# A one-core decoder layer: float32r head sums for the removal keys, later background steps, pinned order of the mixer's products

## The chip, the cores and the metric

One core of a Trainium2 chip runs the whole kernel. The metric is device time in microseconds of one execution. The kernel before takes 2249.39 us, the median of 3 runs (2248.35 to 2249.53).

## The reference, cut to what matters

One layer works on x of 256 tokens by 2048 features, all float32:

```python
x = x + 0.5 * swiglu(rms_norm(x, ffn1_norm), w_gate, w_up, w_down)   # D_FF = 5632
x = gated_parallel_mixer(x, ...)
x = memory_cross_attention(x, mem, ...)
x = x + 0.5 * swiglu(rms_norm(x, ffn2_norm), w_gate, w_up, w_down)
return rms_norm(x, final_norm)
```

The mixer multiplies the normed x by `w_in`, splits the columns into attention, rwkv and gates, and merges both branches:

```python
y_attn = sliding_window_attention(q, k, v, sinks)      # 16 heads of 64, window 128
kk = k * k_k
kk = kk / max(sqrt(sum(kk * kk, over a head)), 1e-12)  # the removal keys
k = k * (1 + (a - 1) * k_a)
y = rwkv7_scan(r, decay, k, v, -kk, kk * a)
y_rwkv = (group_norm(y) * ln_w + ln_b + bonus) * g
merged = gate_attn * (y_attn @ w_proj_attn) + gate_rwkv * (y_rwkv @ w_proj_rwkv)
return x + merged @ w_out
```

## The kernel before

Engines are named as the profile names them: PE multiplies matrices, DVE is VectorE, ACT ScalarE, POOL GpSimd, SP the queue that starts most DMAs.

**Products.** Every float32 operand of a weight product is a pair of float32r values, hi and lo. `times()` (L470) issues three matmuls for each 128x512 block: x hi by w hi (L473), x hi by w lo (L474), x lo by w hi (L475). `product()` walks over the depth in units of two 128-row blocks (KU = 2); for each unit it takes the next weights, then for both token halves (t) calls `multiply()` (L477), which is two times `times()`, six matmuls, and then one `bg.tick()`. With `skew`, the last units run first for one half and then for the other, without ticks. `next_item()` divides the weights up to two items ahead: SP loads raw units (four buffers), ACT casts to hi (L396), DVE subtracts to lo (L397), three buffers each. `feat()` transposes tokens to features on PE (L661), `split()` writes a hi/lo pair (L666, L667, the pairs yahi/yalo, yrhi/yrlo, xhi/xlo among them). PSUM has three small pools (acc, mm, tr) through which everything goes.

**The background.** All else in the mixer is written as generators, held in groups (`Interleave`, L56). A tick lets the first one or few generators of each group run to their next `yield`; `idle(n)` yields n times. So the source decides, tick by tick, behind which product matmuls each step's instructions stand in the engines' queues, which are served in order. In the order of the mixer:

- `attend()` (scores, exp, scaling L936, transposes L942, copies to pt L945, sums L950, then ya's split L957 and L958);
- `scaled()` (L847) evicts a product to tokens, `shifted()` transposes them and mixes each column with its predecessor (L982); the block named "small" holds the low-rank columns;
- `removal_keys(h)` for two halves of eight heads: kk (L1074), its square (L1076), two sums over heads by a matmul with the block matrix `bdones` (L1081), sqrt (L1082), maximum (L1084), two reciprocals (L1086), kk scaled (L1088), at (L1092), bt (L1097, L1099), k (L1104), then the matmuls of `lt` (L1118), masked (L1124) and stored to DRAM (`ld`);
- `substitute()` loads the diagonal blocks (`dl`, L1139, four DMAs on SP) and inverts 32x32 triangles by 31 pairs of DVE steps (L1146, L1151);
- four gate blocks: sigmoid (L1168), the attention product `pa`, and its eviction into `ga` (L1171), stored by POOL;
- `receptances()` and `values()` (kh and kl through `halves_of()` L852, L853/L854; `head_sums()` L857, L861; vtok L1205);
- `pairs(h, q)`, the chain: masks by `masked()` (matmuls L1249, DVE mask L1255) in three sets, `mk`, `later`, `mk_next`, and between them the sums L1286, L1301, L1313, L1329, L1345 to L1357;
- `finish(h, i)`: head sums of y squared, sqrt (L1400), reciprocal (L1402), gate matmuls (L1408), scaling (L1412 to L1419), split into yr;
- gate blocks of rwkv (L1441), the product over yr, the merge, the product with `w_out` and its eviction (L1480), from which `n3.block()` takes the cross-attention's norm.

Sums of weights for the second feed-forward are prepared in the same stretch by `stage()`: two loads on SP (L376), four DVE subtractions (L380 to L385), two stores on SP (L388). `at["pool"]` is None in the mixer and set in both feed-forwards. kh, kl, mk, ga, vtok and the stage's su and sg share one ring of 23 buffers (`t4`).

**The end.** In the second feed-forward the last two of the four output blocks come from plain products; each is evicted on DVE (L769), and `done2()` squares it on ACT (L1587) and multiplies the first three blocks by the final gain on POOL (L1589). `rstd()` (L707, L708, L710) and the last scaling (L1601 to L1605) end the kernel.

Of the kernel before, what the change touches and what calls it, by code (L numbers as in the profile page):

```python
# [7 lines left out]
F32 = mybir.dt.float32  # L8
F32R = mybir.dt.float32r
# [6 lines left out]
P = 128  # L16
# [120 lines left out]
def decoder_layer(ctx: ExitStack, tc: tile.TileContext, a: dict, out: bass.AP):  # L137
# [38 lines left out]


# [17 lines left out]
    def mixer_constants(sp):  # L195
# [36 lines left out]
        return abias, mask3, mask_l, bdup, center, bdones, ones_r, keep  # L232
# [98 lines left out]
    at = {"item": 0, "product": 0, "pool": None}  # L331
# [138 lines left out]
    def times(o, x, w, first, last, **how):  # L470

        (xh, xl), (hi, lo) = x, w
        pe.matmul(o, xh, hi, start=first, stop=False, **how)  # L473
        pe.matmul(o, xh, lo, start=False, stop=False, **how)  # L474
        pe.matmul(o, xl, hi, start=False, stop=last, **how)  # L475

    def multiply(o, x, u, k, t, nk):  # L477
        s = slice(t * P, (t + 1) * P)
        for i in range(KU):
            times(  # L480
                o, [x.at(p, k + i)[:, s] for p in range(2)], [w[:, i, :] for w in u],
                k + i == 0, k + i == nk - 1,
            )
# [230 lines left out]
    def feed_forward(sp, x, norm: Norm, wg, wu, wd, done, begin_last=lambda: None, last=False):  # L714
# [13 lines left out]
        for gi, (j0, nj) in enumerate(GROUPS):  # L728
# [35 lines left out]
            for n in (0, 2):  # L764
                if last and end and n:
                    for m in (n, n + 1):
                        pd = product(h, wd, skew=m == 3)
                        for t in range(2):
                            dve.scalar_tensor_tensor(  # L769
                                col(t, m), pd[t][:], 0.5, col(t, m), ALU.mult, ALU.add  # L770
                            )
                        done(m)
                    continue
                down(sp, h, ch, wd, [[col(t, n + i) for i in range(2)] for t in range(2)])
                if end:
                    done(n)
                    done(n + 1)
# [12 lines left out]
    def aligned(sp):  # L790

        sp.tile([P, 16], F32, name="shift")
# [35 lines left out]
    with tc.tile_pool(name="mx", bufs=1, reuse_waits="tile") as sp:  # L828
        aligned(sp)
        abias, mask3, mask_l, bdup, center, bdones, (bdones_r, bdmean), keep = mixer_constants(sp)  # L830
# [138 lines left out]
        def shifted(tok, cols, mus, outs, name):  # L969
            for q in range(0, len(cols), 2):  # L970
# [96 lines left out]
        def removal_keys(h):  # L1067
# [9 lines left out]
            yield  # L1077
            for i in (0, 2):
                b = tr()
                sq2 = sq[:, i : i + 2, :].rearrange("p c t -> p (c t)")  # L1080
                pe.matmul(b[:], bdones[:], sq2, start=True, stop=True)  # L1081
                act.activation(sq2, b[:], AF.Sqrt)  # L1082
                yield
                dve.tensor_scalar(sq2, sq2, 1e-12, None, ALU.max)  # L1084
                for k in range(2):
                    dve.reciprocal(sq[:, i + k, :], sq[:, i + k, :])  # L1086
                    yield from idle(2)
# [23 lines left out]
            for c in range(2):  # L1111
# [18 lines left out]
                yield  # L1130
# [3 lines left out]
        def substitute():  # L1134
            yield from idle(4)
# [28 lines left out]
        for n in range(4):  # L1164
# [4 lines left out]
            pa = product(ya, W["w_proj_attn"])  # L1169
# [23 lines left out]
        def values(h):  # L1193
# [13 lines left out]
            for i in (0, 2):  # L1207
                b = head_sums(
                    bdones_r, [v[:, i : i + 2, :].rearrange("p c t -> p (c t)") for v in kp[h]]
# [52 lines left out]
        def pairs(h, q):  # L1262
# [11 lines left out]
            for c in range(2):  # L1274
                cs_ = slice(c * P, (c + 1) * P)
                if c == 0:
# [3 lines left out]
                    yield  # L1280
# [58 lines left out]
                if c == 0:  # L1339
                    mk_next = masked(h, js, ((0, 1), (1, 1)))  # L1340
                    yield
# [132 lines left out]
        for n in range(4):  # L1474
# [6 lines left out]
            bg.spawn("feat", n3.block(n, s))  # L1481
# [75 lines left out]
    with tc.tile_pool(name="f2", bufs=1, reuse_waits="tile") as sp:  # L1557
        aligned(sp)
# [15 lines left out]

        def reload():
# [6 lines left out]
        ss = stat.tile([P, 2, 4], F32, tag="ss", name="ss")  # L1582

        def done2(n):
            for t in range(2):
                xs = x[:, t, n * 512 : (n + 1) * 512]
                act.activation(junk_t[:], xs, AF.Square, accum_out=ss[:, t, n : n + 1])  # L1587
                if n < 3:
                    pool.tensor_tensor(xs, xs, fin(n), ALU.mult)  # L1589
# [4 lines left out]
        )  # L1594
        for t in range(2):
# [43 lines left out]
```

## Time and profile before

| | before |
|---|---|
| median of 3 runs | 2249.39 us |
| the profiled execution's own time | 2248.79 us |
| its span | 2247.1 us |
| PE busy | 2231.4 us, 99% |
| DVE busy | 1820.5 us, 81% |
| ACT busy | 1245.0 us, 55% |
| POOL busy | 134.9 us, 6% |
| mean clock granted to PE | 0.999 |
| DMA | 461.35 MB, 205 GB/s over the span |

A row of the timeline has the start in us from the span's beginning, the duration in us, the engine, the line, the operation, output<-inputs with their shape, and how many instructions the row joins; in brackets stands the idle time of the engine before it and what ended it. The waits view has the waiting engine with what it writes and its line, the engine and line it waited for, and then the sum of us, the number and the longest.

### The profile page before, as it was taken

Reading aid. Unit: us, or ns where it says so; the run is one execution under the profiler, and the core shown is the slowest. Engines: PE = TensorE matmul, PEld = TensorE weight load, DVE = VectorE, ACT = ScalarE, POOL = GpSimd, SP = SyncE. Lnnn points to the kernel's source line nnn. Section 1 sums busy time; section 2 is a strip of 40 time slices with the busy share of each in tenths; the row PEclk is TensorE's granted clock in tenths of the full one; section 3 lists DMA queues with packets and bytes.
Section 4 is the critical chain, followed back from the end, with each engine's and each line's share of the span. In section 5 each row is a group of like instructions: output and inputs, shape, how many; then the busy total and the mean of one; then the engine's idle time right before and its main releaser. Section 6 shows DMA issues by size and latency. Waiting matters only on the chain.

```text
span 2247.1 us, 28239 instructions
## 1 busy us (share of the span) xinstructions
PE 2231.4 (99%) x10587; PEld 1833.6 (82%) x10587; DVE 1820.5 (81%) x2342; ACT 1245.0 (55%) x1621; POOL 134.9 (6%) x192
## 2 busy tenths in 40 slices
PE   9999999999999999999999999999999999999998
PEld 7888888888888877788888888888888888888886
DVE  7898988998989476977656666547999999999997
ACT  6555555555556567544444446456665466555654
POOL 1000000000001000201320040001000000000002
PEclk9999999999999999999999999999999999999999
DMA  7555555556556544676767576547565566556564
GB/s 264 187 201 197 201 198 202 200 188 212 195 193 201 169 135 150 198 231 207 224 214 263 187 258 227 190 167 272 197 237 204 195 231 218 201 205 221 197 229 146
DMA packets 229225, 461.35 MB, mean 205 GB/s; under 512 B 15227, under 2 KB 17504, under 8 KB 229088
## 3 DMA queue, kind: packets, MB, share of 16 engines
q1 hardware_dynamic: 220512, 433.62, 56.8%
q0 software_dynamic: 8112, 25.12, 3.5%
q8 instruction: 83, 1.36, 0.2%
q10 hardware_dynamic: 464, 0.79, 0.1%
q14 instruction: 54, 0.44, 0.1%
HBM read 435.91 MB, written 23.59 MB: 204 GB/s over the span
## 4 chain that ended last, share of the span: by engine, by line
PE 95%; DVE 2%; DMA 1%; issue 1%; ACT 1%; SPq 0%; POOL 0%; POOLq 0%; DVEq 0%; ACTq 0%
PE acc L473 19%; PE acc L474 19%; PE acc L475 19%; PE mm L475 8%; PE mm L474 8%; PE mm L473 8%; PE tr L661 2%; PE tr L474 2%; PE tr L473 2%; PE tr L475 2%; PE mm L1313 1%; DVE lo L397 1%; PE tr L1249 1%; DMA raw<-in_w_out_dram 0%; PE mm L903 0%
## 5 line engine op out<-in xcount | busy, mean ns | idle before, releaser
L396 ACT CAST hi<-raw 128x1024 fp32r<-128x1024 f32 (+1 forms) x770 | 756.5, 992 | 714.4 <-PE acc L475 514.8
L397 DVE TENSOR_TENSOR lo<-raw,hi 128x1024 fp32r<-128x1024 f32 (+1 forms) x770 | 886.1, 1153 | 315.5 <-ACT hi L396 314.0
L473 PE MATMUL acc<-hi,xhi 128*128 128x512 f32 (+1 forms) x1166 | 462.2, 397 | 2.1 <-ACT xhi L688 1.7
L474 PE MATMUL acc<-lo,xhi 128*128 128x512 f32 (+1 forms) x1166 | 452.7, 388 | 0.0
L475 PE MATMUL acc<-hi,xlo 128*128 128x512 f32 (+1 forms) x1166 | 452.5, 388 | 0.0
L473 PEld LDWEIGHTS acc<-hi,xhi 128*128 128x128 f32 x1166 | 219.4, 188 | 49.8 <-issue 4.0
L475 PEld LDWEIGHTS acc<-hi,xlo 128*128 128x128 f32 x1166 | 218.8, 188 | 46.0 <-DVE xlo L689 1.0
L474 PEld LDWEIGHTS acc<-lo,xhi 128*128 128x128 f32 x1166 | 219.2, 188 | 43.8 <-issue 1.7
L404 ACT CAST thi<-raw 128x1024 fp32r<-128x1024 f32 x192 | 199.9, 1052 | 62.9 <-DVE raw L427 42.4
L405 DVE TENSOR_TENSOR tlo<-raw,thi 128x1024 fp32r<-128x1024 f32 x192 | 232.2, 1219 | 1.1 <-ACT thi L404 0.4
L474 PE MATMUL acc<-lo,hhi 128*128 128x512 f32 x372 | 145.5, 391 | 0.8 <-DVE lo L397 0.8
L475 PE MATMUL acc<-hi,hlo 128*128 128x512 f32 x372 | 145.5, 391 | 0.0
L473 PE MATMUL mm<-hi,xhi 128*128 128x512 f32 x370 | 145.4, 393 | 0.0
L473 PE MATMUL acc<-hi,hhi 128*128 128x512 f32 x372 | 144.9, 390 | 0.0
L475 PE MATMUL mm<-hi,xlo 128*128 128x512 f32 x370 | 144.3, 390 | 0.0
L474 PE MATMUL mm<-lo,xhi 128*128 128x512 f32 x370 | 144.2, 390 | 0.0
L474 PEld LDWEIGHTS acc<-lo,hhi 128*128 128x128 f32 x372 | 69.9, 188 | 15.4 <-DVE lo L397 1.2
L473 PEld LDWEIGHTS acc<-hi,hhi 128*128 128x128 f32 x372 | 69.9, 188 | 14.3
L475 PEld LDWEIGHTS mm<-hi,xlo 128*128 128x128 f32 x370 | 69.4, 188 | 14.6
L475 PEld LDWEIGHTS acc<-hi,hlo 128*128 128x128 f32 x372 | 69.9, 188 | 14.0
L474 PEld LDWEIGHTS mm<-lo,xhi 128*128 128x128 f32 x370 | 69.5, 188 | 14.2
L473 PEld LDWEIGHTS mm<-hi,xhi 128*128 128x128 f32 x370 | 69.5, 188 | 14.0
(396 smaller groups left out, 3595.7 us busy)
## 6 DMA issues: line engine op xcount, KB each, us to landing
raw<-in_ffn_w_down_dram SPq DMA_DIRECT2D x88, 1024.0 KB, 5.1
raw<-in_ffn_w_gate_dram SPq DMA_DIRECT2D x84, 1024.0 KB, 5.1
raw<-in_ffn_w_up_dram SPq DMA_DIRECT2D x78, 1024.0 KB, 6.2
raw<-in_w_in_dram SPq DMA_DIRECT2D x136, 512.0 KB, 3.5
raw<-in_w_out_dram SPq DMA_DIRECT2D x32, 512.0 KB, 4.4
raw<-sums SPq DMA_DIRECT2D x20, 512.0 KB, 6.3
raw<-in_w_proj_attn_dram SPq DMA_DIRECT2D x16, 512.0 KB, 4.4
raw<-in_w_proj_rwkv_dram SPq DMA_DIRECT2D x16, 512.0 KB, 4.8
```

Of the source, the lines that this page charges most:

```text
L396: at["hi"] = act.copy(hi[:, s], raw[:, s])
L397: at["lo"] = dve.tensor_tensor(lo[:, s], raw[:, s], f32(hi[:, s]), ALU.subtract)
L404: act.copy(hi[:], v[:])
L405: dve.tensor_tensor(lo[:], v[:], f32(hi[:]), ALU.subtract)
L473: pe.matmul(o, xh, hi, start=first, stop=False, **how)
L474: pe.matmul(o, xh, lo, start=False, stop=False, **how)
L475: pe.matmul(o, xl, hi, start=False, stop=last, **how)
L661: pe.transpose(b[:, o : o + P], tok[:, t, col : col + P], ident[:])
L1249: pe.matmul(b[e][:, o : o + P], x1[r, j, cs_], x2[r, j, cs_], start=True, stop=True)
L1313: pe.matmul(vb[:, (o + k) * P : (o + k + 1) * P][:, r], lhs(k, e), rhs[:, k, r], start=first and k + e == 0, stop=True, **ek,)
```

## The change

- The removal keys' squares are split into sh and sl (`halves_of`), and the sums over heads are taken with `head_sums` and the float32r `bdones`, two float32r matmuls in place of one float32 matmul. The float32 `bdones` isn't returned any more. Two ticks pass between the square and the sums, where it was one.
- `shifted()` begins two ticks later for "small". After each store of `lt` two ticks pass in place of one. `substitute()` begins ten ticks after its turn in place of four.
- In `pairs()`, two ticks in place of one pass after `later` and after `mk_next`.
- `multiply()` issues each group of three matmuls after the last matmul of the group before, while `at["pool"]` is None: the order in which the mixer's products are traced is kept.
- The fourth attention product `pa` is skewed. `n3.block()` begins two ticks later.
- In the second feed-forward's last block the eviction goes in halves of 256 columns; ACT squares the first half, DVE the second, into a fifth slot of `ss`, which lies now in the pool's `shift` tile. The gain multiplies are background steps, three ticks later.

```diff
@@ -174,6 +174,10 @@
         for _ in range(n):
             yield
 
+    def later_by(n, steps):
+        yield from idle(n)
+        yield from steps
+
 
     ones = cpool.tile([P, P], F32, name="ones")
     pool.memset(ones[:], 1.0)
@@ -229,7 +233,7 @@
             r = sp.tile([P, P], F32R, name="ones_r" + str(len(ones_r)))
             act.copy(r[:], v[:])
             ones_r.append(r)
-        return abias, mask3, mask_l, bdup, center, bdones, ones_r, keep
+        return abias, mask3, mask_l, bdup, center, ones_r, keep
 
     sinks = cpool.tile([P, 16], F32, name="sinks")
 
@@ -328,7 +332,7 @@
     raws, parts, summed = {}, {}, {}
     first_unused = {items[i][0][1] for i in staged}
     sums_d = dram.tile([len(staged), P, 4, 512], F32, name="sums")
-    at = {"item": 0, "product": 0, "pool": None}
+    at = {"item": 0, "product": 0, "pool": None, "w": None}
 
     def load(u, pieces=None):
 
@@ -472,15 +476,18 @@
         (xh, xl), (hi, lo) = x, w
         pe.matmul(o, xh, hi, start=first, stop=False, **how)
         pe.matmul(o, xh, lo, start=False, stop=False, **how)
-        pe.matmul(o, xl, hi, start=False, stop=last, **how)
+        return pe.matmul(o, xl, hi, start=False, stop=last, **how)
 
     def multiply(o, x, u, k, t, nk):
+
         s = slice(t * P, (t + 1) * P)
         for i in range(KU):
-            times(
-                o, [x.at(p, k + i)[:, s] for p in range(2)], [w[:, i, :] for w in u],
-                k + i == 0, k + i == nk - 1,
-            )
+            with tc.issue_after(at["w"].ins) if at["w"] else nullcontext():
+                w = times(
+                    o, [x.at(p, k + i)[:, s] for p in range(2)], [w[:, i, :] for w in u],
+                    k + i == 0, k + i == nk - 1,
+                )
+            at["w"] = w if at["pool"] is None else None
 
     def combinations(sp, x: Act, seven, name, ready=lambda: True, early=True, n=0):
 
@@ -763,13 +770,18 @@
 
             for n in (0, 2):
                 if last and end and n:
+
+                    whole = [(t, slice(0, 512)) for t in range(2)]
+                    parts_ = [(t, slice(c, c + 256)) for t in range(2) for c in (0, 256)]
+                    pieces = {2: whole, 3: parts_}
                     for m in (n, n + 1):
                         pd = product(h, wd, skew=m == 3)
-                        for t in range(2):
+                        for t, cs in pieces[m]:
                             dve.scalar_tensor_tensor(
-                                col(t, m), pd[t][:], 0.5, col(t, m), ALU.mult, ALU.add
+                                col(t, m)[:, cs], pd[t][:, cs], 0.5, col(t, m)[:, cs],
+                                ALU.mult, ALU.add,
                             )
-                        done(m)
+                            done(m, t, cs)
                     continue
                 down(sp, h, ch, wd, [[col(t, n + i) for i in range(2)] for t in range(2)])
                 if end:
@@ -789,7 +801,7 @@
 
     def aligned(sp):
 
-        sp.tile([P, 16], F32, name="shift")
+        return sp.tile([P, 16], F32, name="shift")
 
 
     with tc.tile_pool(name="f1", bufs=1, reuse_waits="tile") as sp:
@@ -827,7 +839,7 @@
 
     with tc.tile_pool(name="mx", bufs=1, reuse_waits="tile") as sp:
         aligned(sp)
-        abias, mask3, mask_l, bdup, center, bdones, (bdones_r, bdmean), keep = mixer_constants(sp)
+        abias, mask3, mask_l, bdup, center, (bdones, bdmean), keep = mixer_constants(sp)
 
         def t4(name, shape=(P, 4, T), dt=F32):
             return sp.tile(list(shape), dt, tag="t4", name=name, bufs=N4)
@@ -967,6 +979,8 @@
 
 
         def shifted(tok, cols, mus, outs, name):
+            if name == "small":
+                yield from idle(2)
             for q in range(0, len(cols), 2):
                 n = len(cols[q : q + 2])
                 b = feat(tok, cols[q : q + 2])
@@ -1074,11 +1088,13 @@
                 act.activation(kk[:, i, :], kt[h][:, i, :], AF.Copy, scale=nk_k[:, c : c + 1])
             yield
             act.activation(sq[:], kk[:], AF.Square)
-            yield
+            sp_ = halves_of(sq[:], t4("sh", dt=F32R)[:], t4("sl", dt=F32R)[:])
+            yield from idle(2)
             for i in (0, 2):
-                b = tr()
                 sq2 = sq[:, i : i + 2, :].rearrange("p c t -> p (c t)")
-                pe.matmul(b[:], bdones[:], sq2, start=True, stop=True)
+                b = head_sums(
+                    bdones, [v[:, i : i + 2, :].rearrange("p c t -> p (c t)") for v in sp_]
+                )
                 act.activation(sq2, b[:], AF.Sqrt)
                 yield
                 dve.tensor_scalar(sq2, sq2, 1e-12, None, ALU.max)
@@ -1127,12 +1143,12 @@
                     )
                 o = h * 16 + c * 8
                 pool.dma_start(ld[:, o : o + 8, :], lt[:])
-                yield
+                yield from idle(2)
             yield
 
 
         def substitute():
-            yield from idle(4)
+            yield from idle(10)
             dl = t4("dl", (P, 32, 32))
             for i in range(4):
                 q = slice(32 * i, 32 * i + 32)
@@ -1166,7 +1182,7 @@
             g = t4("ga", (P, 2, 512))
             for t in range(2):
                 act.activation(g[:, t, :], pg[t][:], AF.Sigmoid, scale=n2.r[t])
-            pa = product(ya, W["w_proj_attn"])
+            pa = product(ya, W["w_proj_attn"], skew=n == 3)
             for t in range(2):
                 dve.tensor_tensor(g[:, t, :], pa[t][:], g[:, t, :], ALU.mult)
             pool.dma_start(blk(md, n), g[:])
@@ -1206,7 +1222,7 @@
                 yield
             for i in (0, 2):
                 b = head_sums(
-                    bdones_r, [v[:, i : i + 2, :].rearrange("p c t -> p (c t)") for v in kp[h]]
+                    bdones, [v[:, i : i + 2, :].rearrange("p c t -> p (c t)") for v in kp[h]]
                 )
                 v2 = vv[:, i : i + 2, :]
                 dve.tensor_tensor(v2, b[:].rearrange("p (c t) -> p c t", c=2), v2, ALU.mult)
@@ -1277,7 +1293,7 @@
                     mk = masked(h, js, ((0, 0), (1, 0)))
                     yield
                     later = masked(h, js, ((2, 0), (2, 1)))
-                    yield
+                    yield from idle(2)
                 vp = [vtok[h][:, c, j * P : (j + 1) * P] for j in js]
                 x, rr = xb[h, c]
                 b = tr()
@@ -1338,7 +1354,7 @@
                 yield
                 if c == 0:
                     mk_next = masked(h, js, ((0, 1), (1, 1)))
-                    yield
+                    yield from idle(2)
                 b = tr()
                 if c:
                     for k, j in enumerate(js):
@@ -1478,7 +1494,7 @@
             po = product(mt, W["w_out"])
             for t in range(2):
                 dve.tensor_tensor(s[:, t, :], po[t][:], s[:, t, :], ALU.add)
-            bg.spawn("feat", n3.block(n, s))
+            bg.spawn("feat", later_by(2, n3.block(n, s)))
             if n == 0:
                 bg.spawn("mem", memory())
 
@@ -1555,7 +1571,7 @@
 
 
     with tc.tile_pool(name="f2", bufs=1, reuse_waits="tile") as sp:
-        aligned(sp)
+        room = aligned(sp)
         at["pool"] = sp
         x = sp.tile([P, 2, D], F32, name="x")
         fins = []
@@ -1572,6 +1588,11 @@
                 pool.dma_start(fin(n), a["final_norm"][cb].unsqueeze(0).broadcast_to([P, 512]))
                 yield
 
+        def gained(t, n):
+            yield from idle(3)
+            xs = x[:, t, n * 512 : (n + 1) * 512]
+            pool.tensor_tensor(xs, xs, fin(n), ALU.mult)
+
         def reload():
             for n in range(4):
                 cb = slice(n * 512, (n + 1) * 512)
@@ -1579,19 +1600,27 @@
                 pool.dma_start(x[:, :, cb], blk(x3d, n))
 
         bg.spawn("const", reload())
-        ss = stat.tile([P, 2, 4], F32, tag="ss", name="ss")
-
-        def done2(n):
-            for t in range(2):
-                xs = x[:, t, n * 512 : (n + 1) * 512]
-                act.activation(junk_t[:], xs, AF.Square, accum_out=ss[:, t, n : n + 1])
+        ss = room[:, :10].rearrange("p (t n) -> p t n", t=2)
+
+        def done2(n, t=None, cs=slice(0, 512)):
+            for t in range(2) if t is None else (t,):
+                xs = x[:, t, n * 512 : (n + 1) * 512][:, cs]
+                if cs.start:
+                    dve.scalar_tensor_tensor(
+                        junk_t[:, cs], xs, 1.0, xs, ALU.mult, ALU.mult, accum_out=ss[:, t, 4:5]
+                    )
+                else:
+                    act.activation(
+                        junk_t[:, cs], xs, AF.Square, accum_out=ss[:, t, n : n + 1]
+                    )
                 if n < 3:
-                    pool.tensor_tensor(xs, xs, fin(n), ALU.mult)
+                    bg.spawn("ew", gained(t, n))
 
         feed_forward(
             sp, x, n4, W["ffn2_w_gate"], W["ffn2_w_up"], W["ffn2_w_down"], done2,
             begin_last=lambda: bg.spawn("const", gain()), last=True,
         )
+        bg.drain()
         for t in range(2):
             r = rstd(ss[:, t : t + 1, :])[0]
             for n in range(4):
```

## The prediction

> **What bounds the kernel now.** I read the page's span and busy times first, then the chain that ended last, then the PE engine's waits, then windows of the timeline around each place the diff touches.
>
> ```profile
> span 2247.1 us, 28239 instructions
> PE 2231.4 (99%) x10587; PEld 1833.6 (82%) x10587; DVE 1820.5 (81%) x2342; ACT 1245.0 (55%) x1621; POOL 134.9 (6%) x192
> PE 95%; DVE 2%; DMA 1%; issue 1%; ACT 1%; SPq 0%; POOL 0%; POOLq 0%; DVEq 0%; ACTq 0%
> ```
>
> PE is busy 99% of the span and 95% of the chain is PE, so only two things count: what PE executes, and the moments when it stands. What the change can remove of the second kind is in the waits view (us in total, times, longest):
>
> ```profile
> PE tr L661 <- ACT tok L847: 0.8, 1, 0.8
> PE tr L661 <- DVE x L1480: 0.8, 2, 0.5
> PE acc L473 <- DVE ga L1171: 0.4, 1, 0.4
> PE tr L1249 <- DVE mk L1255: 0.3, 1, 0.3
> PE mm L1118 <- DVE lt L1124: 0.3, 1, 0.3
> PE tr L661 <- DVE yalo L958: 0.3, 1, 0.3
> PE tr L1286 <- DVE mk L1255: 0.2, 1, 0.2
> ```
>
> Eight waits, 3.1 us. The idle time understates them: a 128x512 product matmul shows 0.39 busy but they follow each other every 0.227 us (887.68 to 887.90 below), so each wait first uses up 0.16 that counts as busy. 3.1 + 8 x 0.16 = 4.4 us.
>
> **The change, part by part.** Own time of the profiled execution: 2248.79, span 2247.1; the median of the three runs, 2249.39, is 0.6 above it.
>
> *Sums.* The timeline where the first removal sum runs:
>
> ```profile
> 887.68 0.39 PE L475 MATMUL acc<-hi,xlo 128*128 128x512 f32 x1
> 887.90 1.02 PE L1081 MATMUL tr<-sq,bdones 128*128 128x512 f32 x2
> 888.36 0.80 PE L473 MATMUL acc<-hi,xhi 128*128 128x512 f32 x1
> 889.00 0.40 PE L474 MATMUL acc<-lo,xhi 128*128 128x512 f32 x1
> ```
>
> One fp32 sum is recorded as two passes; with the product matmul behind it, it fills 887.90 to 889.00, 1.10 us, so it costs 1.10 - 0.23 = 0.87. Two float32r matmuls cost 2 x 0.227 = 0.45. Saved: 0.42 x 4 sums = 1.65 us, surely on the path. The Trainium skill (FP8 and Floating Point Precision, TensorE Precision Notes) has true fp32 take four passes through the array; four at 0.227 would be 0.91 and the saving 1.8, so row and rule differ by 0.15 in all. The split adds two ACT casts and two DVE subtracts of 128x1024 (1.05 and 1.22, rows 1108.64 and 1110.86 below). ACT has the room (55%); DVE does not always, which comes back below.
>
> *The eight waits.* Two more ticks ahead of each (a tick comes after every six product matmuls, 1.36 us) cover 0.9 at most. I count all gone: -4.4, between 0 and -4.4.
>
> *What moves.* The built order of the two programs shows that the delays add up along the rwkv chain: substitution six ticks later, the keys' chain up to six, so masks and state steps stand some 12 ticks (16 us) later against the product matmuls, whose own order is now pinned. PE's queue is in order: each chain step is now followed or preceded by other product matmuls than before. I compared chain length and cover at each place.
>
> A, first masks. Before:
>
> ```profile
> 1108.64 1.05 ACT L396 CAST hi<-raw 128x1024 fp32r<-128x1024 f32 x1 [1.66 <-PE acc L475]
> 1109.72 1.23 DVE L397 TENSOR_TENSOR lo<-raw,hi 128x1024 fp32r<-128x1024 f32 x1 [1.49 <-ACT hi L396]
> 1110.86 1.22 DVE L854 TENSOR_TENSOR kl<-kt,kh 128x1024 fp32r<-128x1024 f32 x1
> 1112.00 1.28 DVE L1255 TENSOR_TENSOR mk<-tr,mask 128x512 f32<-128x512 f32 x2
> 1112.74 1.75 PE L1249 MATMUL tr<-rt,kk 64*128 64x128 f32 x16 [0.32 <-DVE mk L1255]
> 1114.46 0.69 DVE L381 TENSOR_TENSOR su<-su 128x512 f32<-128x512 f32 x1
> ```
>
> After, three stage additions (L381, L384, L385) stand between that lo and kl, and the second set of mask matmuls waits for the first mk. From the last product matmul before the masks: cast 1.1, lo 1.15, three additions 1.9, kl 1.15, mk 0.65 = 5.95. Cover: eight mask matmuls and six product matmuls, 3.2 (the sixteen of 1112.74 take 1.75, so eight are 0.9 to 1.9). New wait 2.8; bounds 1.9 and 3.1.
>
> B, last finish. Before, it is long over when the product that needs it starts:
>
> ```profile
> 1264.35 0.69 ACT L1400 ACTIVATE sq<-tr,gneps 128x512 f32<-128x512 f32 x1 [0.76 <-PE tr L861]
> 1265.07 3.35 DVE L1402 RECIPROCAL sq<-sq 128x512 f32<-128x512 f32 x1 [0.22 <-ACT sq L1400]
> 1266.87 1.89 PE L1408 MATMUL tr<-xs,g 128*128 128x256 f32 x8
> 1270.93 0.87 DVE L1419 SCALAR_TENSOR_TENSOR yq<-yq,rv,tr 128x256 f32<-128x256 f32 x2
> 1273.79 0.69 DVE L667 TENSOR_TENSOR yrlo<-yq,yrhi 128x512 fp32r<-128x512 f32 x1 [0.85 <-ACT yrhi L666]
> 1294.47 0.39 PE L473 MATMUL acc<-hi,yrhi 128*128 128x512 f32 x1
> ```
>
> Sqrt to the end of yrlo is 1274.48 - 1264.35 = 10.1, with 20 us in hand. After, the last finish stands inside the product over yr itself: between its head sum and the first matmul that needs its part lie 32 product matmuls and four of L1408, 32 x 0.227 + 1.7 = 8.9. Needed: the 10.1, less 0.9 of waiting for ACT in the last row, plus one more lo (1.15) that now stands in the chain, plus a table load for the sqrt (1.28, row 937.00 below) as a gate sigmoid comes before it: 11.7. Wait 2.8; bounds 2.0 (the load half hidden) and 3.3.
>
> C, second half of the removal keys.
>
> ```profile
> 932.89 1.75 DVE L1086 RECIPROCAL sq<-sq 128x256 f32<-128x256 f32 x1
> 937.00 1.28 ACT L1168 ACT_TABLE_LOAD   x1
> ```
>
> The second sqrt now falls between the two gate sigmoids: three loads in a row instead of one, 3.8, then two reciprocals (3.5) in front of two lo's. Cover from the end of the gate product to the matmul that needs the lo, some 4 to 5 us. Wait 1.1 there, and 0.9 where ga's eviction (L1171) is queued behind kk: 2.0; bounds 0.9 and 3.0.
>
> D, substitution.
>
> ```profile
> 974.73 0.16 DVE L1151 TENSOR_REDUCE xt<-tmp 128x3 f32<-128x9 f32 x1
> 974.93 0.17 DVE L1146 TENSOR_TENSOR tmp<-xt,dl 128x16 f32<-128x16 f32 x1
> 980.10 0.22 DVE L1151 TENSOR_REDUCE xt<-tmp 128x8 f32<-128x64 f32 x1
> ```
>
> The first 15 small steps were spread between four lo's; after, all 15 stand in one run between an eviction and a lo: 15 of 0.20 (974.73 to 974.93) to 0.26 are 3.3, plus lo 1.2 and the eviction 0.65 = 5.2 against 3.0 of product matmuls (13 x 0.227). Queued behind them is that lo, and PE's L474 waits for it. 2.2; bounds 1.5 and 2.4.
>
> E, attention.
>
> ```profile
> 812.90 1.14 DVE L936 TENSOR_SCALAR s<-s,den 128x256 f32<-128x256 f32 x4
> 814.87 1.07 ACT L945 COPY pt<-tr 128x512 f32<-128x512 f32 x2 [0.97 <-PE tr L942]
> 815.83 0.91 ACT L847 ACTIVATE tok<-acc,rs 128x288 f32<-128x288 f32 x2
> ```
>
> The token copy no longer stalls its transposes (in the eight above), but the two score blocks' transposes now stand together without product matmuls between them, and the sums behind them need both copies (1.07) after the last scaling (814.04). 1.1 for the copies and about as much for the scaling: 2.3; bounds 1.1 and 3.0.
>
> F, small ones (L1118 behind a 1.2 us DVE step, evictions behind a lo): 1.3; bounds 0 and 1.6.
>
> *Queues.* On SP the four dl loads come seven raw loads later and the stage's loads and stores earlier against the chain; they have the substitution's six ticks (8 us) as cover, so 0. Without it they cost a landing, 3 us. That is a rival.
>
> *Norm steps, tail.* n3's two ticks are in the eight. At the end:
>
> ```profile
> 2208.94 7.76 DVE L397 TENSOR_TENSOR lo<-raw,hi 128x1024 fp32r<-128x1024 f32 x4
> 2210.28 4.21 POOL L1589 TENSOR_TENSOR x<-x,raw 128x512 f32<-128x512 f32 x2 [0.26 <-ACT junk L1587]
> 2238.46 0.69 DVE L769 SCALAR_TENSOR_TENSOR x<-acc,x 128x512 f32<-128x512 f32 x1 [0.30 <-PE acc L475]
> 2239.94 0.16 DVE L707 TENSOR_REDUCE ms<-ss 128x1 f32<-128x4 f32 x1 [0.79 <-ACT junk L1587]
> ```
>
> Eviction to reduce takes 1.48; two evictions and a square of 128x256 I estimate at 0.44 each (half of the 0.87 for the two of L1419), 1.4 with gaps: -0.1, bounds -0.4 and +0.2. The gain multiplies stand in POOL's order where they stood, behind the same squares, so "later" has nothing to move: 0. Four lo's beside them take 7.76, where four at 1.15 (1109.72 to 1110.86) would take 4.6. The Trainium skill (SBUF — State Buffer, Who interferes with whom) says why they may: a DVE instruction with two SBUF inputs and a GpSimd one that reads SBUF lock each other out of a shared port. The rows agree, but no queue changes.
>
> *Sum.* New waits 2.8 + 2.8 + 2.0 + 2.2 + 2.3 + 1.3 = 13.4; gone 4.4 + 1.65 + 0.1 = 6.15. Net +7.25: 2248.79 + 7.25 = 2256.0. The runs lie up to 0.7 above the profiled one, so 2256.5. With all low bounds (7.4) it is 2250.1, with all high (16.4) 2259.0.
>
> **Rivals.** 0.2%, 4.5 us, is about what a measurement of this kernel can tell from no change.
>
> 1. Waits go and the new chains are hidden. From 2248.79, -6.15: 2242.6. For it: after a stall ACT and DVE have caught up, so the next chain starts with more cover. Against it: in A, B and D the chains are longer than their cover by 2 us and more. 10%.
>
> 2. About half of the new waits come: 2248.8 + 6.7 - 6.15 = 2249.4. For it: A to F are summed one by one, though a wait in C moves the DVE work of D ahead too. 20%.
>
> 3. Slower still: in A the kept buffers of kh and vtok are released by the stage's stores, which now stand on SP behind raw loads. One late landing
>
> ```profile
> raw<-in_w_in_dram SPq DMA_DIRECT2D x136, 512.0 KB, 3.5
> ```
>
> added to A's chain gives 2256.5 + 3.5 = 2260. It decides once a store lands later than A's three additions. 15%.
>
> 4. "Gained later" does move the multiplies, the 7.76 shrinks, and the longer of the two waits for xhi goes:
>
> ```profile
> PE acc L473 <- ACT xhi L688: 1.7, 2, 0.9
> ```
>
> 2256.5 - 0.9 = 2255.6. Against it: POOL's order. It is the case in which the Trainium skill's port rule, named above, would decide. 5%.
>
> **The numbers.** The forecast as it stands has 50%. The likeliest one's own range is 2251 to 2259. The range reaches to 2247, into rival 2, and to 2261.5, for rival 3. Faster 10% (rival 1), same 20% (rival 2), slower 70%.
>
> **What would show it.** Right: the eight waits are missing, and PE's waits name mk L1255 with over 2 us, yrhi or yrlo with over 2 us near the product over yr, and lo behind the substitution's first steps; the sums appear as head sums of 0.39 each. Wrong: those waits stay under 0.5 each, which would mean that DVE runs ahead at these places; or a DMA ends last in A. Wrong too if the product matmuls stand in another order than the built one.

## The result and the profile after

The changed kernel takes 2278.97 us, the median of 4 runs (2276.88 to 2279.95), against 2248.87 for the kernel before on the same chip: 1.0135 of it, 95% interval 1.0123 to 1.0147. Slower, as forecast, but by 30.1 us where 7.3 were forecast; the range ended at 2261.5. The profiled execution took 2276.88, its span 28.0 more than before's.

The head of the changed kernel's page, and then PE's largest waits from the mixer on:

```profile
span 2275.1 us, 28268 instructions
PE 2235.0 (98%) x10587; PEld 1835.7 (81%) x10587; DVE 1830.6 (80%) x2350; ACT 1248.4 (55%) x1624; POOL 132.8 (6%) x192
PE 92%; DVE 3%; DMA 2%; issue 1%; ACT 1%; POOL 0%; POOLq 0%; ACTq 0%; DVEq 0%; SPq 0%
```

```profile
PE tr L1265 <- DVE mk L1271: 14.4, 2, 14.0
PE acc L478 <- DVE lo L401: 4.3, 3, 2.4
PE acc L477 <- ACT yrhi L673: 2.4, 1, 2.4
PE mm L1134 <- DVE lt L1140: 1.7, 1, 1.7
PE tr L954 <- DVE s L948: 1.4, 2, 1.2
PE acc L477 <- DVE ga L1187: 1.1, 2, 0.6
PE acc L477 <- DVE x L1496: 0.9, 1, 0.9
PE tr L1217 <- DVE mk L1271: 0.7, 1, 0.7
PE tr L962 <- ACT pt L957: 0.5, 1, 0.5
PE acc L479 <- DVE yrlo L674: 0.4, 1, 0.4
```

All of PE's waits, the small ones and those of the kernel's start included, add up to 31.4 us, those of before to 7.2: 24.2 of the 28.0 are waits, and one wait is half of it. It stands at the first masks (A of the prediction). Its place in the timeline:

```profile
1148.50 0.48 SPq L392 DMA_DIRECT2D sums<-su  x1
1159.12 1.22 DVE L866 TENSOR_TENSOR kl<-kt,kh 128x1024 fp32r<-128x1024 f32 x1 [9.02 <-DMA sums<-su]
1160.05 1.26 ACT L1457 ACTIVATE gr<-acc,rs 128x512 f32<-128x512 f32 x2 [10.47 <-DMA sums<-sg]
1160.45 1.29 DVE L1271 TENSOR_TENSOR mk<-tr,mask 128x512 f32<-128x512 f32 x2
1161.19 2.67 PE L1265 MATMUL tr<-rt,kk 64*128 64x128 f32 x16 [14.02 <-DVE mk L1271]
1166.53 1.29 DVE L1271 TENSOR_TENSOR mk<-tr,mask 128x512 f32<-128x512 f32 x2 [4.80 <-DMA grd<-gr]
```

Read it backwards. PE stands 14 us for mk. mk is queued on DVE behind kl, and DVE has nothing to compute for 9.0 us: kl's buffer in the common ring was last a stage buffer su, whose store (L392) was issued at 1148.50 and is still being read out. The chain of waits puts that landing at 10.5 us:

```profile
1148.50 10.52 DMA sums<-su
```

ACT waits in the same way for sg's store, and the next mk for gr's. In the built order kl's instruction follows that store without a product matmul between them; before, kl waited for no store at all.

Why a store takes so long, from the windows view (PE, PEld, DVE, ACT, POOL busy, granted clock, DMA share, GB/s), first before, then after:

```profile
1110.00:1120.00 10.00, 9.49 (x65) 7.76 (x63) 8.19 (x11) 4.32 (x8) 0.14 (x1) 1.00 0.91 297
1120.00:1130.00 10.00, 10.00 (x82) 8.73 (x80) 6.83 (x11) 3.92 (x7) 3.29 (x5) 1.00 0.62 217
```

```profile
1130.00:1140.00 10.00, 10.00 (x53) 8.56 (x53) 9.93 (x13) 4.08 (x5) 3.43 (x5) 1.00 1.03 376
1140.00:1150.00 10.00, 7.18 (x42) 5.40 (x40) 7.80 (x10) 3.29 (x4) 8.32 (x14) 1.00 1.06 335
1150.00:1160.00 10.00, 0.00 (x0) 0.00 (x0) 0.98 (x2) 0.00 (x0) 0.00 (x0) 0.58 1.04 324
```

A DMA share of 1 or above means that the engines are full, and they are for 30 us. Stage loads, stage stores, raw loads and the loads of xb and rb, which went out from 1097 to 1106 before the stage began, now meet. The DMA view of 1112 to 1130 before and of 1145 to 1160 after (KB each, median us to landing):

```profile
sums<-su SPq DMA_DIRECT2D x2, 512.0 KB, 3.7
sums<-sg SPq DMA_DIRECT2D x1, 512.0 KB, 7.0
```

```profile
sums<-su SPq DMA_DIRECT2D x2, 512.0 KB, 11.3
sums<-sg SPq DMA_DIRECT2D x2, 512.0 KB, 11.2
```

So the stores take 3.7 and 7.0 us before and 11 after. From 1150 to 1160 the engines move 324 GB/s at the share at which they moved 376 from 1130 to 1140. The small packets of xb and rb may have a part in this (294 under 512 bytes from 1145 to 1160; 172 in the view of before); how large it is wasn't tested.

The second part that the forecast had not: the clock after a wait.

```profile
813.00:816.00 3.00, 2.29 (x12) 1.60 (x13) 2.25 (x7) 1.19 (x3) 0.00 (x0) 0.61 0.32 118
816.00:819.00 3.00, 3.00 (x14) 1.62 (x12) 1.41 (x5) 1.02 (x4) 0.00 (x0) 0.82 0.00 0
996.00:999.00 3.00, 1.98 (x7) 1.56 (x8) 2.93 (x7) 0.00 (x0) 0.00 (x0) 0.83 0.31 77
999.00:1002.00 3.00, 3.00 (x10) 2.41 (x9) 1.83 (x4) 0.65 (x1) 0.00 (x0) 0.60 0.91 283
1161.00:1164.00 3.00, 2.81 (x17) 2.58 (x18) 0.73 (x2) 0.31 (x1) 2.10 (x4) 0.50 1.04 418
1164.00:1167.00 3.00, 2.55 (x8) 1.70 (x8) 0.47 (x1) 0.83 (x1) 0.00 (x0) 0.80 0.83 212
```

After the waits at 811, 994 and 1147 PE runs for 3.4 to 4 us at half its clock; the rows, 3 us each, cut these stretches in two. Busy time times the missing share, row by row, is an estimate of the price: 0.9 + 0.5 + 0.3 + 1.2 + 1.4 + 0.5 = 4.8 us. So 24.2 of waits, 4.8 of clock and 1.7 saved by the sums make 27.3 of the 28.0.

### The profile page after: what moved, and what is told of

The parts are those of the page before. It is cut to its first block, busy times and chain, and to the rows that moved or that the text cites. A ratio compares the mean times of both kernels' runs of the same rounds, so it can differ in the third digit from the quotient of the medians.

```text
span 2275.1 us, 28268 instructions
## 1 busy us (share of the span) xinstructions
PE 2235.0 (98%) x10587; PEld 1835.7 (81%) x10587; DVE 1830.6 (80%) x2350; ACT 1248.4 (55%) x1624; POOL 132.8 (6%) x192
## 4 chain that ended last, share of the span: by engine, by line
PE 92%; DVE 3%; DMA 2%; issue 1%; ACT 1%; POOL 0%; POOLq 0%; ACTq 0%; DVEq 0%; SPq 0%
PE acc L477 19%; PE acc L478 18%; PE acc L479 18%; PE mm L478 8%; PE mm L479 8%; PE mm L477 8%; PE tr L668 2%; PE tr L478 2%; PE tr L477 2%; PE tr L479 2%; PE mm L1329 1%; DVE lo L401 1%; PE tr L1265 1%; DMA raw<-in_w_out_dram 0%; DMA sums<-su 0%
## 5 line engine op out<-in xcount | busy, mean ns | idle before, releaser
L401 DVE TENSOR_TENSOR lo<-raw,hi 128x1024 fp32r<-128x1024 f32 (+1 forms) x770 | 890.6, 1160 | 325.0 <-ACT hi L400 323.3
L477 PEld LDWEIGHTS mm<-hi,xhi 128*128 128x128 f32 x370 | 69.5, 188 | 14.1
L478 PEld LDWEIGHTS mm<-lo,xhi 128*128 128x128 f32 x370 | 69.5, 188 | 14.1
```

The source lines that it names most:

```text
L401: at["lo"] = dve.tensor_tensor(lo[:, s], raw[:, s], f32(hi[:, s]), ALU.subtract)
```

## The experiments

Theory 1 at the start: a store of the stage holds the buffer. Its rivals: the chain's own length, the pinned order, the four new buffers, lateness as such.

**The stage moved as far as the chain.**

```diff
-STAGE_AT = [266 + 2 * n for n in range(10)]
+STAGE_AT = [275 + 2 * n for n in range(10)]
```

> The changed kernel with the stage's steps begun nine items later (108 product matmuls), as far as the chain was moved. Theory 1 (kl, gr and mk take ring buffers whose last reader is a store of the stage that has only just been issued, and wait for it to land): the 14.0 us wait of PE for mk L1271 falls to 3 or less, the time to 2279 - 12 = 2267 or below, the waits for lo and yrhi stay. Rival (the chain of cast, subtraction, three additions and mask is itself too long, or the pinned order puts it there): the wait stays above 10 and the time at 2276 to 2280.

2266.0 us. PE's waits at the masks:

```profile
PE tr L1265 <- DVE mk L1271: 1.2, 2, 1.0
PE tr L1302 <- ACT vtok L1221: 0.9, 1, 0.9
```

12.9 us less, and the other waits stand as they were (lo 4.4, yrhi 2.5, lt 1.7). The chain's own length is not what makes the 14.

**The pinned order taken out.**

```diff
-            with tc.issue_after(at["w"].ins) if at["w"] else nullcontext():
+            with nullcontext():
```

> The changed kernel without the pinned order of the mixer's product matmuls. Theory 1 (store in front of kl): in the built order kl still takes its buffer from a store issued at the same product matmul, so the wait for mk stays near 14 and the time between 2276 and 2282. Rival (the pinned order makes the stall): the wait is gone and the time near 2265.

2268.2 us, outside both expectations. The stall is still there:

```profile
PE tr L1265 <- DVE mk L1271: 11.6, 2, 11.3
PE acc L477 <- ACT yrhi L673: 0.6, 1, 0.6
```

It doesn't need the pin, though it is 2.7 shorter; the waits of the bunched attention transposes (L954, L962) are gone, with the low clock after them, and the wait for yrhi falls from 2.4 to 0.6. The pin costs 10.8 us in this kernel, spread over many places, the stall itself among them.

**The substitution at its old tick.**

```diff
-            yield from idle(10)
+            yield from idle(4)
```

> The changed kernel with the substitution begun after 4 ticks in place of 10. Theory 1: the chain stands 36 product matmuls earlier, kl's store is 24 matmuls (5.4 us) old, so kl's wait falls to about 4; but mk's buffer now comes from a store issued at the same matmul, so a wait of 4 to 10 appears there: 2268 to 2275. Rival (any lateness of the chain costs in proportion, 36 of 108 matmuls): 2270, but without a wait on a store. The waits of the substitution (2.5) and in the product over yr (2.6) should shrink.

2271.6 us. The total came as theory 1 had it, but not the mechanism: kl waits for nothing, and yet

```profile
PE tr L1217 <- DVE mk L1271: 6.2, 1, 6.2
DVE sg L384 <- DMA sg<-in_ffn_w_gate_dram: 6.3, 1, 6.3
```

Here DVE's queue is held by a stage addition (L384) that waits for its load, issued at 1132.6 and landed 12.4 us later, and mk stands behind it. So theory 1 was too narrow: whichever instruction of DVE or ACT depends on a late transfer, as data or as a buffer, holds what is queued behind it. The waits for the substitution's lo and for yrhi are gone, as expected for D and B.

**The removal sums back in fp32.** `halves_of` and `head_sums` out, the fp32 matmul in, ticks kept:

```diff
-            sp_ = halves_of(sq[:], t4("sh", dt=F32R)[:], t4("sl", dt=F32R)[:])
+                pe.matmul(b[:], bdones32[:], sq2, start=True, stop=True)
```

> The changed kernel with the removal sums as before (fp32, without the four buffers sh and sl), all ticks kept. Theory 1 with the ring's turn set by the chain's position: kl still waits for a store issued at the same matmul, 2279 + 1.3 for the dearer sums = 2280. Rival (the four extra buffers turned the ring so that kl falls on a stage buffer): the 14 us go, 2266.

2278.5 us, the wait for mk 14.1. The four buffers are not the cause. The sums' saving doesn't show either.

**Parts alone, from the kernel before.** The float32r sums, with two ticks before them:

```diff
-            yield
+            sp_ = halves_of(sq[:], t4("sh", dt=F32R)[:], t4("sl", dt=F32R)[:])
+            yield from idle(2)
...
-                b = tr()
-                pe.matmul(b[:], bdones[:], sq2, start=True, stop=True)
+                b = head_sums(
+                    bdones_r, [v[:, i : i + 2, :].rearrange("p c t -> p (c t)") for v in sp_]
+                )
```

> The kernel before with the float32r removal sums (with sh and sl, two ticks before them) alone. Theory 1: the chain starts 12 product matmuls later and no mask or key takes a buffer whose store is younger than 11 matmuls (2.5 us), so only the sums' saving shows: 2249.2 - 1.3 = 2247.9, between 2246 and 2250, no wait of PE above 1.5 in the mixer. Rival (the four more buffers and two more subtractions cost by themselves): 2252 or above.

2254.7 us, ratio 1.0030 (1.0019 to 1.0042). The rival's size, by another way. The largest waits of the mixer stand at 975, at the first matmuls of an attention product:

```profile
PE acc L473 <- ACT hi L396: 1.7, 1, 1.7
PE acc L474 <- DVE lo L397: 1.3, 2, 0.8
```

The cast to hi that PE waits for there stands behind the gate's two sigmoids in ACT's queue, which end at 974.4; in the kernel before, two more casts stand ahead of them. Nor could it have begun before 972.9: its raw load landed then, 3.5 us later than before. That load stands in SP's queue behind the four dl loads, and the first of these waits for lt's store to land. SP's wait, before and here:

```profile
SPq L1139 <- DMA ld<-lt: 3.5, 1, 3.5
SPq L1141 <- DMA ld<-lt: 7.1, 1, 7.1
```

So SP's queue too is held by its first instruction that depends on a late transfer. All waits of PE together are 4.1 above before's; what makes the rest of the 6.3 us stays open.

The two ticks after `later` and `mk_next`:

```diff
-                    yield
+                    yield from idle(2)
```

> The kernel before with the two ticks after later and after mk_next alone. The first masks stand where they stood; mk's youngest store is 4 matmuls old as before. Theory 1: within 2 of before, 2247 to 2251, the two waits for mk (0.3 and 0.2) changed by less than 1. Rival (the masks' step is what costs): 2255 or above.

2250.2 us, 1.0007 (0.9997 to 1.0018): nothing that can be told. The ticks at the masks themselves do no harm that shows.

The four delays aimed at single waits:

```diff
+            if name == "small":
+                yield from idle(2)
...
-                yield
+                yield from idle(2)
...
-            pa = product(ya, W["w_proj_attn"])
+            pa = product(ya, W["w_proj_attn"], skew=n == 3)
...
-            bg.spawn("feat", n3.block(n, s))
+            bg.spawn("feat", later_by(2, n3.block(n, s)))
```

> The kernel before with the delays aimed at single waits alone (small two ticks later, two ticks after each store of lt, the fourth attention product skewed, the norm two ticks later). The chain starts 60 product matmuls later; vtok takes a buffer whose store is 5 matmuls (1.1 us) old. Theory 1: a wait for vtok of 2 to 5 us, less the 2.5 us of waits aimed at: 2249 to 2254. Rival (the delays do what they are for): 2246 or below.

2256.9 us, 1.0038 (1.0022 to 1.0054), above both. The waits for the tokens, yalo, lt and ga are gone, but PE waits 4.4 for mk behind a stage addition that waits 5.9 for its load, as with the substitution's old tick, and 1.7 for hi and 0.5 for lo at 974 as with the sums alone (SP waits 7.3 for lt's store there).

The pinned order (`multiply()` and `at["w"]` as in the changed kernel):

```diff
+            with tc.issue_after(at["w"].ins) if at["w"] else nullcontext():
+                w = times(
...
+            at["w"] = w if at["pool"] is None else None
```

> The kernel before with the pinned order of the mixer's products alone. The chain stands where it stood, and the youngest stores too. Taking the pin out of the changed kernel gave 10.8 us back; by theory 1 most of that is the changed kernel's own positions (the stall at the masks, the last finish), and here only the bunched attention transposes (3 us) show: 2250 to 2254. Rival (the pin costs by itself): 2257 or above; or nothing: 2249.

2252.4 us, 1.0016 (1.0006 to 1.0025), inside the expectation for the transposes. The windows after them:

```profile
813.00:816.00 3.00, 1.93 (x8) 1.53 (x8) 2.93 (x10) 1.11 (x3) 0.00 (x0) 0.53 0.31 121
816.00:819.00 3.00, 2.58 (x8) 2.13 (x9) 0.19 (x2) 1.33 (x3) 0.00 (x0) 0.50 0.00 0
```

Part of the cost is the halved clock, 0.9 + 1.3 us here by the same product. Its ten runs spread from 2249.2 (mean clock 0.999) to 2253.4 (0.997).

The substitution after ten ticks:

```diff
-            yield from idle(4)
+            yield from idle(10)
```

> The kernel before with the substitution begun after 10 ticks in place of 4, alone. The chain starts 42 product matmuls later; one mk takes a buffer whose store is 3 matmuls old. Theory 1 (young stores cost): a wait for mk of 3 to 6 us, 2251 to 2256. Rival (the delay is covered by the 20 us that the last finish has in hand): 2248 to 2250.

2248.8 us, 1.0002 (0.9992 to 1.0012). The rival held. One mk does wait 1.7 us for a store of the stage, but no wait of PE hangs on it; the 0.9 that PE waits for another mk stands behind a stage addition that waits 1.1 for its load. The stage's stores land in 4.4 and 5.7 us here (median of su's and of sg's, 1118 to 1138). The age of a store alone says little.

**Both causes out.** No pin, stage at 275:

```diff
-STAGE_AT = [266 + 2 * n for n in range(10)]
+STAGE_AT = [275 + 2 * n for n in range(10)]
...
-            with tc.issue_after(at["w"].ins) if at["w"] else nullcontext():
+            with nullcontext():
```

> The changed kernel without the pinned order and with the stage nine items later. If the two causes are separate, the times subtract: 2268.2 (without the pin) less its 11.3 us wait for mk and 1 to 2 us of clock after it, 2255 to 2258. If they are one cause, the second edit gives nothing: 2266 to 2268.

2254.0 us, 1 us below what was expected for separate causes and 25.0 below the changed kernel. The two edits alone gave 12.9 and 10.8, together 23.7, so they add up within about 1 us. What is left of C, D and lt (2.2 for a lo, 1.4 for lt) keeps it above before, 1.0027 (1.0017 to 1.0037).

**The meeting alone, made in the kernel before.**

```diff
-STAGE_AT = [266 + 2 * n for n in range(10)]
+STAGE_AT = [257 + 2 * n for n in range(10)]
```

> The kernel before with the stage's steps begun nine items earlier, nothing else: the chain meets the stage as it does in the changed kernel, while chain, sums, ticks and order are those of before. If that meeting alone makes the stall (DVE's queue held by an instruction that waits for a stage transfer, at full DMA): a wait of PE of 4 to 14 us near the first masks, 2253 to 2265. If it needs the changed chain, its ticks or the pinned order: 2248 to 2250.

2257.1 us, 1.0038 (1.0023 to 1.0053). The time is as the first expectation had it, the wait is not. DMA is full as in the changed kernel:

```profile
1110.00:1120.00 10.00, 7.90 (x40) 6.50 (x38) 7.53 (x10) 2.24 (x3) 1.86 (x4) 0.87 1.06 301
1120.00:1130.00 10.00, 8.21 (x40) 6.97 (x40) 5.01 (x7) 3.86 (x7) 0.00 (x0) 0.62 0.90 348
```

PE waits only 2.1 for mk, and 1.3 for hi, which waits 7.1 on ACT for its raw load. On DVE nothing waits for a stage transfer: lo, three additions, kl and mk follow each other without a gap, and the 2.1 are that chain's length. The clock is 0.50 from 1117 to 1128, some 4 us by the product used above, about as much as all of PE's waits have grown (4.1). So the meeting costs 8.6 us without the moved chain's ticks and without the pin, but it doesn't make the 14 us wait. That wait stands only in the changed kernel and in those of its variants whose kl waits for a store of su (9.0 us on DVE; 8.7 without the pin, 8.8 with the fp32 sums).

**Parts without harm, put together.** The norm steps and the end alone:

```diff
-            bg.spawn("feat", n3.block(n, s))
+            bg.spawn("feat", later_by(2, n3.block(n, s)))
...
+        def done2(n, t=None, cs=slice(0, 512)):
...
-                    pool.tensor_tensor(xs, xs, fin(n), ALU.mult)
+                    bg.spawn("ew", gained(t, n))
```

> The kernel before with the later norm steps and the whole change of the end alone. Nothing of the chain moves. As the prediction has it: 0.1 at the end, up to 1.1 at the norm, none for the gain multiplies: 2247.5 to 2249.5. Rival (the gain multiplies move): 2246.5 or below.

2247.7 us, 0.9996 (0.9987 to 1.0005). The gain multiplies have not moved against each other: the pair that takes 4.21 us on POOL takes 4.21 again, after the same gap of 0.26. With the float32r sums but one tick, as in before:

```diff
-                pe.matmul(b[:], bdones[:], sq2, start=True, stop=True)
+                b = head_sums(
+                    bdones_r, [v[:, i : i + 2, :].rearrange("p c t -> p (c t)") for v in sp_]
+                )
```

> The kernel before with the float32r sums without the extra tick, the later norm steps and the change of the end. In the built order the chain and the stores stand exactly as before. If only the moved chain made the sums dear: 2248.6 - 1.3 - 0.5 = 2246.8, between 2245.5 and 2248.5. If the four buffers or the two subtractions cost by themselves: 2250 or above.

2247.4 us, 0.9995 (0.9986 to 1.0004). It stays inside what a measurement can tell, though the chain stood still; against 2247.7 without the sums, little of the 1.65 is left. The two traces, compared from one product matmul to the next, show where it goes. By 938 us, by the start of the same product matmul in both, the kernel with the float32r sums is 1.35 us ahead of the one without; by 975 it has lost 0.5 of that, and at the first masks another 1.2, where the wait for mk at L1286 of before rises from 0.2 to 0.9. The saving is made and then waited away. And with the stage nine items later:

```diff
-STAGE_AT = [266 + 2 * n for n in range(10)]
+STAGE_AT = [275 + 2 * n for n in range(10)]
```

> The kernel before with the float32r sums (no extra tick), the later norm steps and the change of the end, and with the stage nine items later. If the stage's transfers cost the masks something even before (waits of 0.8 to 1.6 for mk): 2245 to 2247. If not: 2247 to 2248.5, as without the shift.

2252.6 us, 1.0020 (1.0010 to 1.0029): worse. The stage now falls beside the product over yr. The DMA share there is 1.04 from 1270 to 1280 and 1.03 from 1280 to 1290 (0.74 and 0.85 without the shift), casts wait up to 4.3 us for their raw loads, and four lo's and one eviction are late for PE (2.1 and 1.6). No version was found that beats before beyond the interval.

## Why the prediction was wrong, step by step

- **A**, 2.8 us with bounds 1.9 and 3.1: measured 14.0, and 0.7 at the next mask. This step failed. The prediction summed casts, additions and the mask, but took kl's buffer as free. The mechanism stood in rival 3, with "one late landing" priced at 3.5, the median of the 136 raw loads of w_in; the landing in question took 10.5. Its condition, a store that lands later than the three additions, was met at once, and so was the prediction's own sign of being wrong, that a DMA ends last in A. That the chain as such was well summed shows in the kernel with the stage at 257, where the same additions stand ahead of kl, no transfer holds DVE and PE waits 2.1.
- **Queues**, "so 0": right for the dl loads. Behind the substitution's six ticks they cost nothing; without these ticks, with the sums alone and with the four delays alone, they delay raw loads by some 3 us and have a part in 2.2 us of waits (not in the changed kernel with the substitution at its old tick). For the stage's loads and stores it is part of the same failed step: they were counted on SP's queue and not in the DMA engines, which they filled.
- **What moves**, "some 12 ticks (16 us)": mis-sized. In the built order the first mask stands 108 product matmuls later, 18 ticks or 24.5 us. That is what brought the chain into the stage's time.
- **The clock** was in no term: 4.8 us.
- **The eight waits**, "I count all gone": mostly right. At their own places tokens, yalo, ga and the two waits for mk went. The norm's wait did not: its transposes no longer wait, but the product matmul behind the same eviction does, 0.9 (0.8 before). Where the first lt matmuls waited 0.3 for lt, they wait 0.3 for kk.
- **F**, 1.3 with bounds 0 and 1.6: 1.7, a little above them, for lt in the second half of the keys. The DVE step ahead of it, a lo, took 3.12 us in place of 1.2, beside POOL's multiply of kt,

```profile
958.00 3.12 DVE L401 TENSOR_TENSOR lo<-raw,hi 128x1024 fp32r<-128x1024 f32 x1
957.67 2.37 POOL L1124 TENSOR_TENSOR kt<-kt,aa 128x1024 f32<-128x1024 f32 x1 [31.38 <-DVE aa L1120]
```

  which the port rule that the prediction cited from the Trainium skill covers (SBUF — State Buffer, Who interferes with whom), at another place than the one it was weighed for.
- **B**, 2.8: 2.4 for yrhi and 0.4 for yrlo. Right in place and size; gone in the kernel with the substitution at its old tick, and 0.6 in the one without the pin.
- **C**, 2.0: 1.2 for a lo (the 4.3 less D's 2.4 and 0.8 near the end, which stood before too) and 0.6 for ga; another 0.5 for ga stands in the first half of the keys. Right.
- **D**, 2.2: 2.4, the largest of the waits for lo, behind a run of 13 small steps (3.2 us). Right, without its clock.
- **E**, 2.3: 1.4 for the scaling, 0.5 for the copies and 0.3 more. Right; the kernel with the pin alone shows the scaling's 1.4 too. But it comes from the pinned order, not from the delays, and the prediction did not price the pin as a part.
- **Sums**, -1.65: the passes went as forecast (float32r matmuls of 0.39 in place of the fp32 pairs). In the times of the whole kernel the gain didn't show in either pair of runs: in the pair compared above, 1.35 us are saved and then waited away.
- **Tail**, -0.1, and the gain multiplies, 0: right. The last eviction (L780) to the last reduce takes 2268.01 - 2266.68 = 1.33, before 1.48.

```profile
2266.68 0.76 DVE L780 SCALAR_TENSOR_TENSOR x<-acc,x 128x256 f32<-128x256 f32 x2 [0.51 <-PE acc L479]
2268.01 0.16 DVE L714 TENSOR_REDUCE ms<-shift 128x1 f32<-128x5 f32 x1
```

## What to carry to other kernels

When a step moves, look up the last reader of the buffers that it takes and the transfers around its new place: a landing must be priced at the DMA load there (a store took 3.7 to 7.0 us at a share of 0.62 to 0.91, 11 at 1.05), not at its median. In a queue served in order it isn't the moved step's own data that decides, but the first instruction ahead of it that depends on a transfer. And a wait of PE of one to two microseconds can cost again that much in clock.

## What was not expected of the hardware

The granted clock fell after waits far shorter than the 14 us one: to 0.61 and 0.82 after two waits for scaling of 0.2 and 1.2 us, and to 0.83 and 0.60 after one of 2.37. After another of 2.41, in the product over yr, it stayed at 1.00.

The trace shows what sets the two cases apart. The clock is 1.00 or 0.50 and nothing between. In the changed kernel's mixer it is 0.50 from 813.64 to 817.05, from 997.96 to 1001.37 and from 1151.56 to 1165.21, that is for 3.41 us twice and then for four times as long. The starts are 184.32 and 153.60 us apart, 54 and 45 times 3.413: they lie on one grid. (So does a fourth stretch at the start, from 8.10 to 11.51, 236 steps before the one at 813.64. It costs nothing: the 60th product matmul starts at 26.4 in both kernels.) These are the steps of that grid before the first two drops, and the two steps around the wait without a drop:

```profile
810.23:813.64 3.41, 1.97 (x11) 1.12 (x10) 2.36 (x13) 2.64 (x12) 0.00 (x0) 1.00 0.88 285
994.55:997.96 3.41, 1.04 (x5) 0.80 (x5) 3.03 (x9) 0.96 (x1) 0.00 (x0) 1.00 0.26 97
1325.63:1329.04 3.41, 2.19 (x10) 1.50 (x8) 3.41 (x6) 1.60 (x2) 0.00 (x0) 1.00 0.77 258
1329.04:1332.45 3.41, 1.87 (x7) 1.26 (x8) 2.22 (x4) 0.62 (x1) 0.00 (x0) 1.00 0.71 225
```

The wait of 2.37 lies inside one step: PE is busy for 1.04 of 3.41 us, and the next step is at half clock. The wait of 2.41 is divided between two steps, with 2.19 and 1.87 busy, and nothing follows. In the kernel with the sums back in fp32 the grid lies elsewhere, with drops at 962.68 and 1331.32. There it is the other way round: the wait for yrhi (2.40) lies inside one step, with 0.93 busy, and the clock falls; the wait at 995.7 (2.07) is divided, and it doesn't. So whether such a wait costs clock depends on where it falls against the grid. That is luck, and it can be a part of the spread among the ten runs with the pin alone.

The Trainium skill (TensorE: Matmul & The Clock Gate, Part 1: The HAM clock gate) has the clock halved after at least one idle window of about 3.4 us, windows that run freely. The grid agrees with the free windows. But PE need not stand for a whole window: 1.04 us busy of 3.41 were few enough. In the step before the first drop PE was busy for longer, 1.97, than in a step without a drop, 1.87, but mostly with transposes:

```profile
811.13 0.91 PE L954 MATMUL tr<-ident,s 128*128 128x128 f32 x4 [0.23 <-DVE s L948]
813.25 1.73 PE L954 MATMUL tr<-ident,s 128*128 128x128 f32 x8 [1.21 <-DVE s L948]
```

The same page (Part 4: PE-mode transpose) says that transposes don't count as busy in the way of other matmuls. This fits the first drop, but a run that separates the transposes from the waits wasn't tried; at 994 only product matmuls stand on both sides of the wait, so there they can't be the reason.
